# Block 1's modulation vectors: from TensorE matmuls to multiply-and-sum on VectorE, with layer A's first projections advanced tile by tile

## The chip, the core and the metric

The kernel runs on one NeuronCore of a Trainium2 chip. The metric is the device time of one execution in microseconds; three runs of the kernel before gave 2185.78, 2187.06 and 2189.66 us, median 2187.06. Everything else here comes from one profiled execution.

## The reference, cut to what matters

Two transformer blocks on 256 tokens of width 1024, in fp32. Block 1 has a forgetting-attention layer (A), a mixture of experts, a latent-attention layer (B) and a second mixture of experts. Every sublayer's input is an RMS norm that is scaled and shifted, and its output is gated, by vectors computed from one conditioning vector `c`. These vectors are what the change touches:

```python
c_act = jax.nn.silu(c)                                   # [1, 1024]
for layer in range(2):
    sh1, sc1, g1, sh2, sc2, g2 = split(c_act @ w_mod[layer] + b_mod[layer], 6)   # 6 x 1024
    h = rmsnorm(x, norm_g) * (1 + sc1) + sh1
    x = x + g1 * attention(h)
    h = rmsnorm(x, ffn_norm_g[layer]) * (1 + sc2) + sh2
    x = x + g2 * grouped_moe(h)
# between the layers, for the shared keys and values of layer B:
shift, scale = split(c_act @ kv_w_mod + kv_b_mod, 2)     # 2 x 1024
```

Block 2 works the same way with two conditioning vectors (latent and context), which stay as they are.

## The kernel before, in words

Activations are feature-major: `x` is [128 partitions, 8 tiles, 256 tokens]. Weights stream from HBM in units of [128, 1024] fp32 (512 KB) through one ring of eight buffers `raw`; all these loads are issued by SyncE's queue (L335). A linear layer runs in split precision: `wsplit` (L346) makes of each unit a rounded part H on ScalarE (L356) and a remainder L on VectorE (L357), and `lin` (L371) does three matmuls for each of eight tiles of the contraction (L379 to L381).

A modulation is a vector times a matrix. `mods` (L547) does 2048 columns as 16 units: each unit meets `crep`, the activated vector spread over 32 columns, in four matmuls, one to each quarter of the array (L556; each shows as two records in the profile, so 8 records a unit). After 16 units the result is copied (L561), transposed by four matmuls (L564) and added to the bias (L569). One unit is one yield of 1.4.

The order of work is written with generators: `mix` advances several streams in proportion to their yielded amounts against a declared total, and `Chain` strings modulations together so that whoever needs one drives the chain on. In `run` (L1414):

- Layer A: first `drain(mod0([0]))`, the 16 units of shift and scale for layer A's input; then `layer_a` (total 122) mixed with a chain of 80 units (total 115): layer 1's gate and shift group, a group of block 2, the other group of layer 1, another group of block 2, and the group of the shared keys and values.
- Mixture of experts 1: a chain of one group of block 2 and layer 2's first group, then the experts beside the context's work of block 2.
- Layer B: `layer_b` (L1061, total 140) with a chain of layer 2's other 32 units (total 55). Its start is filled with two hidden steps of the context's feed-forward.

`layer_a` (L696) splits `wf` and the first two query tiles ahead, normalises and modulates the whole input (`norm` with `late`, L452, `modulate`, L475), and then runs the three projections one after another, mixed with the chain. The instructions are not issued strictly in the order of the code: the trace has layer A's sums of squares ahead of the first modulation's end, although the code has them after it.

Of the kernel before, what the change touches and what calls it, by code (L numbers as in the profile page):

```python
# [40 lines left out]
# ---------------------------------------------------------------- layout (host)  # L41
# [5 lines left out]
def constants():  # L47
    """Constants that depend on shapes alone: common, of block 1, of block 2, of its even layer."""
# [5 lines left out]
    c1["phalf"] = half  # L54
    c1["ltri"] = (p[:, None] < p[None, :]).astype(np.float32)
    z = np.zeros((P, P))
    c1["causal"] = np.concatenate([z, np.where(p[:, None] >= p[None, :], 0.0, NEG)], 1)
    c1["chunk"] = np.concatenate([z, np.where(p[:, None] // 64 >= p[None, :] // 64, 0.0, NEG)], 1)
    c1["delta"] = (p[:, None] % 32 == np.arange(16)[None, :]).astype(np.float32)
# [31 lines left out]
    return cat(c0), cat(c1), cat(c2), cat(c3)  # L91


(C0_OFF, C0), (C1_OFF, C1), (C2_OFF, C2), (C3_OFF, C3) = constants()
# [15 lines left out]
def kunits(w, kt):  # L110
    """[K, M] -> [K/(128*kt), 128, kt*M]."""
# [5 lines left out]
def modunits(w):  # L117
    """[1024, C] -> [C/2048, 8, 2, 128, 1024]: columns 256*(2j+h).. of four column groups j."""
# [4 lines left out]

def vunits(w):
    """[1024, M] -> [M/256, 2, 128, 4*256]: halves of the contraction."""
# [6 lines left out]
    ("c", 8), ("c2", 8), ("cc2", 8),  # L132
# [13 lines left out]
def layout(i):  # L146
# [6 lines left out]
    for r in range(0, P, 32):  # L153
        bf[r:r + 16, 0] = g["a_b_f"][0]
    vec = {
        "c": cols(g["c"][0]), "c2": cols(g["c_2"][0]), "cc2": cols(g["c_ctx_2"]),
# [18 lines left out]
    # layer A  # L175
# [20 lines left out]
    # layer B  # L196
# [5 lines left out]
    # experts  # L202
# [4 lines left out]
    # block 2, even layer: heads in pairs (i of kv head 0, i of kv head 1)  # L207
# [9 lines left out]
    # block 2, odd layer  # L217
# [12 lines left out]
    o["cst3"] = C3  # L230
    return o
# [32 lines left out]
def upto(n, g):  # L264
    """as much of a generator as amounts to n."""
# [22 lines left out]
class Net:  # L288
# [163 lines left out]
    def norm(self, x, kt, g, sc, sh, dh=None, dl=None, keep=None, save=None, late=False):  # L452
        """rms norm of x [128, kt, 256], times g*(1+sc), plus sh; in parts to dh, dl, or whole to keep; late: sc and sh
        come after x."""
        if late:
            self.modulate(self.normed(x, kt), self.gains(kt, g, sc), sh, dh, dl)
            return
# [1131 lines left out]
```

## Time and profile before

| | us |
|---|---|
| median of three runs | 2187.06 |
| span of the profiled execution | 2181.0 |
| TensorE busy in it | 2045.4 (94%) |
| VectorE busy | 1194.1 (55%) |
| ScalarE busy | 826.0 (38%) |
| GpSimd busy | 138.1 (6%) |
| mean DMA rate | 226 GB/s |

The page gives the span from the first to the last instruction; the execution's own device time is not listed beside it, so the median stands for it, 6.06 us (0.28%) above the span. Busy shares are averages over stages with different limits; the table of stretches says which engine is full where. By the stretches, layer A lies in 0 to about 240 us, the first mixture of experts up to about 700, layer B up to about 915, the second mixture up to about 1290, and block 2 follows.

### The profile page before, as it was taken

The numbers are of one execution on the slowest core, as the hardware profiler recorded it, in microseconds if no ns is written. First come the engines' busy times: TensorE is split into PE (matmuls) and PEld (weight loads), VectorE is DVE, ScalarE is ACT, GpSimd is POOL, SyncE is SP. The second block draws the span as 40 slices with busy tenths as digits, with TensorE's granted clock in tenths as the row PEclk, the third lists the DMA queues.
The fourth block names the chain that finished last, engine by engine and source line by source line (L and its number), as shares of the span: only waits on it lengthen the run. The fifth ranks groups of instructions, "written<-read, shape, count | busy, mean of one in ns | idle before, by whom it ended". The sixth has DMA issues, their size and how long they took to land.

```text
span 2181.0 us, 35834 instructions
## 1 busy us (share of the span) xinstructions
PE 2045.4 (94%) x13942; PEld 1482.8 (68%) x13942; DVE 1194.1 (55%) x3145; ACT 826.0 (38%) x1532; POOL 138.1 (6%) x152
## 2 busy tenths in 40 slices
PE   5999889999998999989999999997999999998999
PEld 3666654444445877783555448766999877768999
DVE  3644643333244676761233247867777555576776
ACT  2443323333123455541121134665444434444443
POOL 1000200000002020100000013102000100001000
PEclk8999889999999999999999999998999999998999
DMA  9788677758787566447877996302655443324552
GB/s 374 267 304 311 248 261 308 267 214 328 293 347 280 203 224 223 144 166 314 360 287 298 409 359 215 134 21 79 211 184 173 158 145 115 113 102 135 185 186 95
DMA packets 135848, 492.87 MB, mean 226 GB/s; under 512 B 15136, under 2 KB 15536, under 8 KB 135408
## 3 DMA queue, kind: packets, MB, share of 16 engines
q1 hardware_dynamic: 134640, 487.63, 61.4%
q8 instruction: 114, 1.87, 0.3%
q10 hardware_dynamic: 864, 2.53, 0.3%
q0 software_dynamic: 160, 0.27, 0.1%
q14 instruction: 70, 0.57, 0.1%
HBM read 489.32 MB, written 1.05 MB: 225 GB/s over the span
## 4 chain that ended last, share of the span: by engine, by line
PE 49%; DVE 3%; ACT 1%; DMA 1%; issue 1%; POOL 0%; SPq 0%; POOLq 0%; ACTq 0%; DVEq 0%
PE psL L379 8%; PE psL L381 8%; PE psL L380 8%; PE psE L931 6%; PE psE L949 2%; PE psM L556 1%; PE psS L1381 1%; PE psT L636 1%; PE psS L1276 1%; PE psD L379 1%; PE psD L381 1%; PE psD L380 1%; PE psV L614 1%; PE psL L393 1%; PE psL L395 1%; PE psL L394 1%
## 5 line engine op out<-in xcount | busy, mean ns | idle before, releaser
L379 PE MATMUL psL<-hh,H 128*128 128x256 f32 (+1 forms) x1800 | 533.8, 298 | 14.4 <-ACT H L356 6.1
L381 PE MATMUL psL<-hh,L 128*128 128x256 f32 (+1 forms) x1800 | 524.2, 293 | 5.3 <-DVE L L357 5.3
L380 PE MATMUL psL<-hl,H 128*128 128x256 f32 (+1 forms) x1800 | 523.2, 292 | 4.1 <-DVE hl L483 3.8
L357 DVE TENSOR_TENSOR L<-raw,H 128x1024 fp32r<-128x1024 f32 (+1 forms) x336 | 410.3, 1225 | 183.0 <-ACT H L356 181.3
L356 ACT CAST H<-raw 128x1024 fp32r<-128x1024 f32 (+1 forms) x336 | 347.1, 1039 | 390.3 <-PE psL L380 123.1
L379 PEld LDWEIGHTS psL<-hh,H 128*128 128x128 f32 x1800 | 350.0, 195 | 58.1 <-issue 25.3
L381 PEld LDWEIGHTS psL<-hh,L 128*128 128x128 f32 x1800 | 348.4, 194 | 32.0 <-issue 16.4
L380 PEld LDWEIGHTS psL<-hl,H 128*128 128x128 f32 x1800 | 349.2, 194 | 15.4 <-issue 4.5
L931 PE MATMUL psE<-eraw,xg 128*64 128x512 f32 x512 | 155.1, 617 | 8.5 <-PEq L997 8.5
L436 POOL TENSOR_TENSOR sa<-sa,sq 128x256 f32<-128x256 f32 x83 | 76.7, 924 | 1215.7 <-ACT sq L434 1210.0
L931 PE MATMUL psE<-raw,xg 128*64 128x512 f32 x512 | 145.3, 603 | 0.0
L556 PE MATMUL psM<-raw,crep 128*32 128x256 f32 x1408 | 126.2, 408 | 15.9 <-DVE crep L606 13.7
L589 ACT ACTIVATE pr<-psS,nm,hr 128x512 f32<-128x512 f32 (+1 forms) x96 | 67.7, 706 | 100.4 <-DVE nm L583 57.8
L949 PE MATMUL psE<-raw,at 128*64 128x512 f32 x384 | 100.0, 599 | 5.4 <-ACT at L943 5.3
L379 PE MATMUL psL<-ah,H 128*128 128x256 f32 x296 | 87.1, 297 | 4.8 <-DVE x L1165 1.3
L380 PE MATMUL psL<-al,H 128*128 128x256 f32 x296 | 84.3, 285 | 0.7 <-DVE al L369 0.7
L381 PE MATMUL psL<-ah,L 128*128 128x256 f32 x296 | 83.8, 284 | 0.3 <-DVE L L357 0.3
L931 PEld LDWEIGHTS psE<-eraw,xg 128*64 128x64 f32 x512 | 38.7, 139 | 64.7 <-issue 54.0
L580 DVE TENSOR_REDUCE mx<-psS 128x1 f32<-128x512 f32 (+1 forms) x80 | 46.1, 580 | 58.6 <-PE psS L1276 44.4
L556 PEld LDWEIGHTS psM<-raw,crep 128*32 128x32 f32 x1408 | 38.9, 113 | 54.9 <-issue 16.5
L931 PEld LDWEIGHTS psE<-raw,xg 128*64 128x64 f32 x512 | 37.0, 136 | 54.2 <-issue 45.2
L955 DVE SCALAR_TENSOR_TENSOR mh<-psE,wsl,mh 128x512 fp32r<-128x512 f32 x32 | 23.3, 747 | 82.5 <-ACT mh L954 82.0
(404 smaller groups left out, 3474.8 us busy)
## 6 DMA issues: line engine op xcount, KB each, us to landing
raw<-in_mod_dram SPq DMA_DIRECT2D x192, 512.0 KB, 4.8
raw<-in_ed_dram SPq DMA_DIRECT2D x96, 512.0 KB, 8.3
raw<-in_fg_dram SPq DMA_DIRECT2D x66, 512.0 KB, 4.4
raw<-in_fu_dram SPq DMA_DIRECT2D x66, 512.0 KB, 4.2
raw<-in_fo_dram SPq DMA_DIRECT2D x66, 512.0 KB, 4.1
eraw<-in_eg_dram SPq DMA_DIRECT2D x64, 512.0 KB, 7.7
raw<-in_eg_dram SPq DMA_DIRECT2D x64, 512.0 KB, 9.2
raw<-in_eu_dram SPq DMA_DIRECT2D x64, 512.0 KB, 7.6
```

The lines of the kernel that those rows point to most:

```text
L356: nc.scalar.copy(h[:, :n], r[:, :n])
L357: nc.vector.tensor_tensor(l[:, :n], r[:, :n], h[:, :n].bitcast(F32), op=ALU.subtract)
L379: mm(ps[:, ns], wh, xh[:, k, ns], start=k == 0, stop=False)
L380: mm(ps[:, ns], wh, xl[:, k, ns], start=False, stop=False)
L381: mm(ps[:, ns], wl, xh[:, k, ns], start=False, stop=k == kt - 1)
L436: (nc.vector if i else nc.gpsimd).tensor_tensor(acc[i], acc[i], sq, op=ALU.add)
L556: nc.tensor.matmul(ps[32 * j:32 * j + 32, 256 * hf:256 * hf + 256], crep[:, k, :], r[:, 256 * j:256 * j + 256], start=k == 0, stop=k == KD ...
L580: V.reduce_max(mx, ps[:, :n], axis=AX.X)
L589: nc.scalar.activation(p, ps[:, :n], AF.Exp, bias=nm, scale=scale, accum_out=sm)
L931: nc.tensor.matmul(ps[64 * j:64 * j + 64, :], xg[:, 2 * q + k, sl[j]], r[j][:, 512 * k:512 * k + 512], start=q + k == 0, stop=q + k == 4)
L949: nc.tensor.matmul(py[hf][64 * j:64 * j + 64, :], at[:, k, 64 * j:64 * j + 64], r[j][:, 512 * hf:512 * hf + 512], start=k == 0, stop=k == 3)
L955: V.scalar_tensor_tensor(yl[:, fs], py[hf], wsl[:, pr:pr + 1], yh[:, fs].bitcast(F32), op0=ALU.mult, op1=ALU.subtract)
```

## The change

All seven groups of block 1 (16 units each, 112 units) leave `mods`. The host stores these weights transposed, so that a unit [128, 1024] holds 128 output features on partitions and the whole contraction along the free dimension; the bytes are the same. A new `rowmods` multiplies each such row unit by the activated vector, which is broadcast to all partitions once, sums it, scales it and adds the bias in one VectorE instruction with an accumulator output, straight into the column of the modulation vector. The norm gains are folded into bias and scale (`gained`), so `norm` gets the finished gain.

```diff
+def rows(w):
+    return np.ascontiguousarray(w.T).reshape(-1, P, D)
...
-    o["mod0"] = modunits(g["w_mod"][0])
-    o["mod1"] = modunits(g["w_mod"][1])
-    o["modkv"] = modunits(g["kv_w_mod"])
+    o["crow"] = np.ascontiguousarray(g["c"].reshape(1, D))
+    o["mod0"] = rows(g["w_mod"][0])
+    o["mod1"] = rows(g["w_mod"][1])
+    o["modkv"] = rows(g["kv_w_mod"])
...
+    def rowmods(self, src, tiles, out, bias, gain=None):
+        V = self.nc.vector
+        for f in tiles:
+            r = self.wload(src[f])
+            one = slice(f, f + 1)
+            sc = 1.0 if gain is None else gain[:, f % KD:f % KD + 1]
+            V.tensor_tensor_reduce(r, r, self.crow, op0=ALU.mult, op1=ALU.add, scale=sc,
+                                   scalar=bias[:, one], accum_out=out[:, one])
+            yield 1.4
+
+    def gained(self, bias, at, g):
+        b = bias[:, at:at + KD]
+        self.nc.vector.scalar_tensor_tensor(b, b, 1.0, g, op0=ALU.add, op1=ALU.mult)
```

Layer A's 16 first row units alternate scale and shift, feature tile by feature tile; then each tile of the input is modulated and all three first projections take one step of the contraction with it (in PSUM banks of kinds V and L):

```diff
-        self.ahead(*((w, KD, P) for w in (a["wf"], a["wqk"][0], a["wqk"][1])))
-        self.norm(self.x, KD, self.v["ang"], m0[:, 8:16], m0[:, 0:8], xh, xl, late=True)
+        self.consts(self.st, "csta", CA, CA_OFF)
+        z = self.normed(self.x, KD)
+        firsts = [(a["wf"], "V"), (a["wqk"][0], "L"), (a["wqk"][1], "L")]
+        ws, pss = [], []
+        for k in range(KD):
+            drain(self.rowmods(a["mod0"], (KD + k,), m0, self.v["bm0"], self.v["ang"]))
+            drain(self.rowmods(a["mod0"], (k,), m0, self.v["bm0"]))
+            if k < len(firsts):
+                ws.append(self.wsplit(firsts[k][0], KD, P))
+                pss.append(self.psum(firsts[k][1]))
+        for k in range(KD):
+            self.modulate(z[k:k + 1], m0[:, KD + k:KD + k + 1], m0[:, k:k + 1], xh[:, k:k + 1], xl[:, k:k + 1])
+            for w, ps in zip(ws, pss):
+                self.lin_k(ps, *(v[:, k] for v in w), xh, xl, k, KD)
         yield 4.0
-        ps = self.lin(self.wsplit(a["wf"], KD, P), KD, xh, xl, S)
+        ps = pss.pop(0)
...
-                ps = self.lin(self.wsplit(a["wqk"][2 * u + m], KD, P), KD, xh, xl, S)
+                ps = pss.pop(0) if pss else self.lin(self.wsplit(a["wqk"][2 * u + m], KD, P), KD, xh, xl, S)
```

`lin_k` is one step of `lin`'s loop. The chains are dealt out anew: block 2's second group (on TensorE) moves from layer A to the first mixture of experts, the keys' and values' vectors move to the experts, and all of layer 2's vectors are made in layer B:

```diff
-            self.crep = self.silu_cols(["c"], self.b1)
+            self.crow = self.b1.tile([P, D], F32, name="crow")
+            nc.sync.dma_start(self.crow, a["crow"].partition_broadcast(P))
+            nc.scalar.activation(self.crow, self.crow, AF.Silu)
...
-                chain = Chain(("gate", mod0([1])), ("c0", mod20([0])), ("m0", mod0([2])), ("c1", mod20([1])),
-                              ("kv", self.mods(a["modkv"], [0], self.crep, self.v["bkv"], mk)))
-                drain(mod0([0]))
+                chain = Chain(("gate", mod0(2)), ("c0", mod20([0])), ("m0", mod0(3)), ("m0", mod0(4, v["ffng0"])),
+                              ("m0", mod0(5)))
...
-                drain(mix((self.layer_a(m0, chain), 122), (chain.run(), 115)))
+                drain(mix((self.layer_a(m0, chain), 122), (chain.run(), 67)))
...
-                chain = Chain(("c2", mod20([2])), ("m1", mod1([0])))
+                chain = Chain(("c1", mod20([1, 2])))
...
-                drain(mix((experts, 196), (then(con, cffn.run(1)), 76)))
+                drain(mix((experts, 196), (then(con, cffn.run(1)), 76), (then(kvmod(0), kvmod(1, v["kvng"])), 23)))
...
-                chain = Chain(("m1", mod1([1, 2])))
-                drain(mix((self.layer_b(mk, m1, chain, cffn.run(3)), 140), (chain.run(), 55)))
+                chain = Chain(("in", mod1(0)), ("in", mod1(1, v["bng"])), ("m1", mod1(2)), ("m1", mod1(3)),
+                              ("m1", mod1(4, v["ffng1"])), ("m1", mod1(5)))
+                drain(mix((self.layer_b(mk, m1, chain, cffn.run(3)), 140), (chain.run(), 67)))
```

In `layer_b`, a `yield from chain.run("in")` stands just before layer B's input is scaled. In the diff `mod0(t)`, `mod1(t)` and `kvmod(t)` are `rowmods` over eight row units, 1024 features. Some constants get tiles of their own in the layer that needs them, and two scratch tiles of block 2 move to another pool.

## Rows read from the trace of the kernel before

**Rows 1.** The page: busy time of each engine, share of the span, instructions.
```profile
PE 2045.4 (94%) x13942; PEld 1482.8 (68%) x13942; DVE 1194.1 (55%) x3145; ACT 826.0 (38%) x1532; POOL 138.1 (6%) x152
```

**Rows 2.** Stretches: length, then busy us of each engine, clock, DMA share, GB/s.
```profile
13.70:32.20 18.50, 13.77 (x140) 6.68 (x140) 2.48 (x13) 2.24 (x6) 5.07 (x7) 0.82 1.03 410
32.20:55.00 22.80, 16.31 (x128) 11.18 (x128) 15.52 (x40) 11.46 (x18) 0.00 (x0) 0.78 1.01 397
60.00:240.00 180.00, 172.45 (x1480) 125.16 (x1484) 94.96 (x270) 71.06 (x152) 5.75 (x6) 0.99 0.80 289
330.00:700.00 370.00, 358.36 (x1726) 173.39 (x1722) 140.42 (x408) 118.97 (x239) 10.22 (x12) 1.00 0.77 296
700.00:750.00 50.00, 46.21 (x371) 41.27 (x371) 28.94 (x53) 14.98 (x21) 7.75 (x9) 0.97 0.56 187
750.00:800.00 50.00, 48.87 (x405) 43.09 (x405) 46.06 (x94) 27.04 (x49) 11.48 (x12) 1.00 0.63 212
800.00:850.00 50.00, 46.51 (x340) 36.16 (x338) 30.79 (x85) 26.77 (x55) 4.69 (x5) 1.00 0.75 243
850.00:915.00 65.00, 63.70 (x457) 49.05 (x456) 48.30 (x187) 34.42 (x97) 2.73 (x2) 1.00 0.44 148
```

**Rows 3.** The same for the modulation matmuls of L556 alone: TensorE, its weight loads.
```profile
60.00:240.00 180.00, 46.67 (x566) 14.60 (x570) 0.99 0.80 289
```

**Rows 4.** TensorE in order of time, layer A: start, us, instruction, count.
```profile
150.52 0.28 PE L395 MATMUL psL<-H,hl 128*128 128x256 f32 x1
150.73 2.37 PE L556 MATMUL psM<-raw,crep 128*32 128x256 f32 x40
153.03 0.33 PE L621 MATMUL psT<-cst,pr 128*128 128x128 f32 x1
...
217.67 0.28 PE L379 MATMUL psL<-oh,H 128*128 128x256 f32 x1
217.78 0.28 PE L380 MATMUL psL<-ol,H 128*128 128x256 f32 x1
217.99 0.64 PE L556 MATMUL psM<-raw,crep 128*32 128x256 f32 x8
218.56 0.39 PE L381 MATMUL psL<-oh,L 128*128 128x256 f32 x1
```

**Rows 5.** VectorE in order of time, layer B.
```profile
755.79 1.22 DVE L357 TENSOR_TENSOR L<-raw,H 128x1024 fp32r<-128x1024 f32 x1
756.93 0.42 DVE L511 TENSOR_TENSOR raw<-raw,psN 128x256 f32<-128x256 f32 x1
...
857.42 0.43 DVE L577 CUSTOM_DVE_ANT_0 psS<-psS,cst 128x256 f32<-128x256 f32 x1
857.76 0.14 DVE L577 DVE_READ_ACCUMULATOR2_ANT mx<- 128x1 f32 x1
857.76 0.95 DVE L357 TENSOR_TENSOR L<-raw,H 128x768 fp32r<-128x768 f32 x1
```

**Rows 6.** Every engine in order of time, the start, to the third projection's read.
```profile
12.84 0.42 ACT L434 ACTIVATE sa<-x 128x256 f32<-128x256 f32 x1 [4.57 <-DMA x<-in_xin_dram]
30.75 0.69 DVE L561 COPY msb<-psM 128x512 f32<-128x512 f32 x1 [8.60 <-PE psM L556]
46.80 0.48 DVE L707 TENSOR_SCALAR fz<-psL,vec 128x256 f32<-128x256 f32 x1 [2.73 <-PE psL L381]
55.13 0.77 ACT L735 ACTIVATE qz<-psL 64x256 f32<-64x256 f32 x2 [3.28 <-PE psL L381]
61.19 0.41 PE L380 MATMUL psL<-hl,H 128*128 128x256 f32 x1
61.40 0.41 PE L381 MATMUL psL<-hh,L 128*128 128x256 f32 x1
```

**Rows 7.** Waits in 60 to 240 us: who waited for whom, us, times, longest.
```profile
ACT pr L589 <- DVE nm L583: 26.5, 14, 5.5
ACT pt L625 <- PE psT L623: 26.1, 15, 3.5
```

More of the change, by code (lines that the diff above doesn't have):

```diff
@@ L89, in cat @@
         return off, np.ascontiguousarray(np.concatenate(cols, 1))
-    return cat(c0), cat(c1), cat(c2), cat(c3)
-(C0_OFF, C0), (C1_OFF, C1), (C2_OFF, C2), (C3_OFF, C3) = constants()
+    return cat(c0), cat(c1), cat(c2), cat(c3), cat(ca), cat(cb)
+(C0_OFF, C0), (C1_OFF, C1), (C2_OFF, C2), (C3_OFF, C3), (CA_OFF, CA), (CB_OFF, CB) = constants()
 def cols(v):
@@ L131 @@
 VEC = [
-    ("c", 8), ("c2", 8), ("cc2", 8),
+    ("c2", 8), ("cc2", 8),
     ("ang", 8), ("kvng", 8), ("bng", 8), ("ffng0", 8), ("ffng1", 8), ("fing", 8),
@@ L230, in layout @@
     o["cst3"] = C3
+    o["csta"] = CA
+    o["cstb"] = CB
     return o
@@ L324, in pools, with consts @@
             setattr(self, n, es.enter_context(self.tc.tile_pool(name=n, bufs=b)))
+    def consts(self, pool, name, v, off):
+        t = pool.tile([P, v.shape[1]], F32, name=self.nm(name))
+        self.nc.scalar.dma_start(t, self.a[name])
+        self.c.update({k: t[:, o:o + w] for k, (o, w) in off.items()})
     def splits(self, es, more, side=None):
@@ L382, in lin, with lin_k @@
         return ps
+    def lin_k(self, ps, wh, wl, xh, xl, k, kt):
+        mm = self.nc.tensor.matmul
+        mm(ps[:, :S], wh, xh[:, k], start=k == 0, stop=False)
+        mm(ps[:, :S], wh, xl[:, k], start=False, stop=False)
+        mm(ps[:, :S], wl, xh[:, k], start=False, stop=k == kt - 1)
     def lin_t(self, ws, kt, n, xh, xl, t0):
@@ L429, in rms @@
         nc = self.nc
-        acc = [self.t(self.sm, [P, S], f"sa{i}", bufs=1) for i in range(len(scales))]
+        acc = [self.t(self.wk if i else self.sm, [P, S], f"sa{i}", bufs=1) for i in range(len(scales))]
         for k in range(kt):
@@ L450, in spread, with norm @@
         return pr[:, :S]
[L452 to L457, printed above, removed]
+    def norm(self, x, kt, g, sc, sh, dh=None, dl=None, keep=None, save=None):
         ga = self.gains(kt, g, sc)
@@ L782, in moe_route @@
         h = self.t(mo, [P, KD, S], "mh")
-        self.norm(x, KD, g, m[:, 32:40], m[:, 24:32], keep=h)
+        self.norm(x, KD, m[:, 32:40], None, m[:, 24:32], keep=h)
         yield 4.0
@@ L1093, in layer_b @@
         self.ahead(*((a["wdq"][m], KD, P) for m in range(2)))
+        yield from chain.run("in")
         z = self.room(KD)
-        self.scale(self.x, KD, self.gains(KD, self.v["bng"], m1[:, 8:16]), z, nc.gpsimd)
+        self.scale(self.x, KD, m1[:, 8:16], z, nc.gpsimd)
         self.affine(z, rs, KD, m1[:, 0:8], xh, xl)
@@ L1460, in run @@
             mk = self.b1.tile([P, 16], F32, name="mk")
-            mod0 = lambda g: self.mods(a["mod0"], g, self.crep, self.v["bm0"], m0)
-            mod1 = lambda g: self.mods(a["mod1"], g, self.crep, self.v["bm1"], m1)
+            v = self.v
+            for b, at, g in (("bm0", 8, "ang"), ("bm0", 32, "ffng0"), ("bkv", 8, "kvng"), ("bm1", 8, "bng"),
+                             ("bm1", 32, "ffng1")):
+                self.gained(v[b], at, v[g])
+            mod0 = lambda t, g=None: self.rowmods(a["mod0"], range(8 * t, 8 * t + 8), m0, v["bm0"], g)
+            mod1 = lambda t, g=None: self.rowmods(a["mod1"], range(8 * t, 8 * t + 8), m1, v["bm1"], g)
+            kvmod = lambda t, g=None: self.rowmods(a["modkv"], range(8 * t, 8 * t + 8), mk, v["bkv"], g)
             with ExitStack() as es:
```

21 lines of the change are left out of this document (11 added, 10 removed).

## The prediction, made before the changed kernel ran

> **What bounds the kernel now.** I read the page first: TensorE is busy 94% of the span, VectorE 55% [rows 1]. An average hides stages, so the table of stretches comes next. In layer A's steady part, 60 to 240 us, TensorE has 172.45 of 180 us and VectorE 94.96; in the experts, 330 to 700, 358.36 of 370 and 140.42; in layer B's four stretches from 700 to 915 together 205.3 of 215 and 154.1 [rows 2]. TensorE is the full engine in all of them. Two places differ. From 13.7 to 55 us the transfers run at 410 and 397 GB/s, a DMA share of about 1, and TensorE is busy about three quarters: the start is bound by loading. And in 750 to 800 us VectorE is busy 46.06 of 50 us: layer B's head is nearly full on both engines. Third, I took the modulation matmuls alone: 46.67 us of TensorE's time in 60 to 240 [rows 3].
>
> **What one unit costs, on either engine.** Removed: a unit of four matmuls. Standing alone between two steps of an accumulation it moves the next matmul from 217.78 to 218.56, 0.78 us where a step is 0.11: 0.67 us. Five in a row take 153.03 - 150.52 - 0.12 = 2.39, or 0.48 each [rows 4]. I take 0.57, between them, since both patterns occur. Added: one VectorE instruction over 1024 elements, in a form that the trace has only narrower. A subtract of 1024 holds the engine 1.14 us, start to start; the multiply-type operation with accumulator, 256 wide, holds it 0.34 and its accumulator read starts together with the next instruction [rows 5]. So 1.14 us a row unit; with the read's 0.14 added to it 1.28 at most. In engine time 1.14 on VectorE replaces 0.57 on TensorE: the exchange pays only where TensorE is the bound and VectorE has room.
>
> **The start: -8 us (-13 to +1).** Before, the sixteen units end at 30.75 us, the forget gates are read at 46.80 and the third projection at 55.13 [rows 6]. After, the bytes ahead of that point are 16 row units (8.39 MB), three weights (1.57), x (1.05), c's broadcast (0.52) and constants (about 0.45): 12.0 MB, 29 us at 410 GB/s, and with the slow first microseconds some 33. VectorE has to do 16 x 1.14 rows, 3 x 1.14 splits, 8 x 0.34 for the norm, 16 x 0.34 for the modulating and about 2 us of small steps: 18.2 + 3.4 + 2.7 + 5.4 + 2 = 32 us. When c's row has landed and passed ScalarE the trace does not show; x, next in line, is first used at 12.84 [rows 6], so VectorE begins between 9 and 13 us and is done at 41 to 45. It, not the loading, is last. Then comes the last tile's nine matmuls. If TensorE keeps up, this is 1 to 2 us (a step is 0.12 us, or 0.21 at the lower clock, as at 61.19 us [rows 6]) and the third projection is ready at 43 to 47. If all 72 matmuls stand behind the row sums, they take 72 x 0.21 = 15 us from about 36, so 51; with 5 us more for a late c row, 56. I take 47: -8. The chain's ten units that ran before 60 us become about six rows, 7 us of VectorE in time that was idle or shorter now.
>
> **Layer A's steady part: -28 us (-38 to 0).** Its window holds 566 records, 71 units; 16 stay on TensorE (block 2's first group), so 36.1 of the 46.67 us go and TensorE keeps 136.4. VectorE gets 32 x 1.14 = 36.5 and has 131.4, with the copies after each group gone (about 3). If TensorE stays as full as it is (172.45 of 180) the window is 142: -38. But VectorE would then be 92% busy, as full as in 750 to 800 us, and its instructions run in order: a row sum stands ahead of splits and of the softmax steps that ScalarE waits for (26.5 us in this window [rows 7]). I take 152 us, TensorE 90% and VectorE 86%. The end at 0 is the case in which the modulations only filled gaps (below). SyncE's queue issues 32 units less here, 16 of them to layer B and 16 to the experts, so loading eases from 289 GB/s.
>
> **First experts: +2 us (0 to +8).** Block 2's group takes the place of layer 2's first group, 16 units for 16. The sixteen key and value rows add 18 us to VectorE's 140.42 of 370, in time that it has idle, and 8.4 MB, which lifts 296 GB/s to 319. They pass through the ring that the experts' weights use, on the same SyncE queue; a row sum whose load is late holds the expert steps behind it on VectorE. 8 us is half a microsecond for each.
>
> **Layer B: +2 us (-18 to +30).** TensorE loses 32 x 0.57 = 18 us, which leaves 187; VectorE gains 48 x 1.14 = 55 and comes to 208.9 of 215. Here VectorE becomes the fuller engine. By stretches, with twelve rows for each 50 us: 42.6 of 50 in 700 to 750 (gain 4, as TensorE allows), 59.8 in 750 to 800 (loss 6 to 10, some rows being done ahead), 44.5 in 800 to 850 (gain 4), about 64 of 65 in the last (0 to +2). The new wait for the input's vectors has little left to do by then: that point is reached after about 39 of 140 declared units, where the chain has made 13 of its 16 rows; the three others cost VectorE 3.4 us in its fullest place, with the scaling on GpSimd and the query-side projections behind them. Worst, a row stands in front of what TensorE needs next all the time: 55 less part of the 18.
>
> **The sum.** -8 - 28 + 2 + 2 = -32 us. The profiled execution's span is 2181.0 us and the median of the runs 2187.06, 0.28% more; I keep those 6.06 us as they are: 2149 for the span, 2155 for the time.
>
> **The rivals.** *All of it comes back* (2118): TensorE bounds every stage and VectorE's rows find idle time; -13 - 38 + 0 - 18 = -69. For it: 94% and 55%. Against: the sum for layer B, 97% of VectorE.
>
> *The modulations were filler* (2183): TensorE without them waits for the softmax chain instead. For it: the five units at 150.73 run just after the values' projection ended and right before the transposes of finished weights [rows 4], and ScalarE waits 26.1 us for transposes, 26.5 us for VectorE [rows 7]. Against: elsewhere units sit between steps at the full pace of 0.12 us, where each one delays the rest. Layer A then gives nothing and the sum is -8 + 0 + 2 + 2 = -4. The Trainium skill speaks for this rival in "Perfetto Trace Analysis", section "Identifying the Most-Contended Engine": matmul busy time does not tell how close TensorE is to its limit, and the weight loads' busy share is the better measure. By that page, the 125.16 us of weight loads in 180 (70%) [rows 2] would leave TensorE headroom in layer A, and the 32 us would shrink to 4.
>
> *VectorE takes over* (2218, the slower side): in layers A and B each of the 80 row sums sits ahead of a split or softmax step that TensorE waits for. Price 80 x 1.14 = 91, less TensorE's relief of 36 + 18, -8 and +2: +31. It decides from the point where VectorE's share goes beyond the 92% of 750 to 800 us, in which TensorE was still busy 48.87 of 50 us. For it: 208.9 of 215 in layer B. Against: that same stretch, and the 131 of 152 in layer A.
>
> *The tiles don't advance together* (2164): the modulating stays behind all sixteen row sums and the projections start as late as now; the start gives +1 and the rest stands.
>
> **How the numbers follow.** Forecast 0.52, all back 0.14, filler 0.17, VectorE 0.12, no advance 0.05. A measurement of this kernel tells about 0.2% (4.4 us) from no change. Filler, at 4 us, is split 0.07 faster, 0.09 same, 0.01 slower; the other cases fall on one side each: faster 0.52 + 0.14 + 0.05 + 0.07 = 0.78, same 0.09, slower 0.13. The time is the forecast's, 2155. The forecast alone spans about 2135 to 2175; for 8 in 10 the range reaches up past the filler to 2190 and down to 2118, which leaves out VectorE's case and half of the first.
>
> **What would show it.** In the profile after: row sums of about 1.14 us from one to the next; 16 of them before about 35 us, and the third projection's read near 47; layer A's output projection over near 205 instead of 240, with VectorE at 85 to 90% and TensorE near 90%; waits of TensorE for the remainder of a split (L357) or for softmax steps grown in layer B, and VectorE above 92% there. The forecast is wrong if TensorE in layer A falls below 85% busy while VectorE stays below it too (filler), if a row sum costs well over 1.3 us, or if TensorE's waits for VectorE add more than 20 us from 700 to 915.

## The result, and the profile after

The changed kernel takes 2219.03 us (median of 2216.17 to 2220.61) against 2187.64 of the kernel before on the same chip: 1.0141 times, 95% interval 1.0127 to 1.0156. The prediction was 2155. The busy line of its page:

```profile
PE 2003.7 (90%) x13018; PEld 1485.1 (67%) x13018; DVE 1312.8 (59%) x3354; ACT 828.9 (37%) x1532; POOL 141.9 (6%) x152
```

Against [rows 1] TensorE has 41.7 us less to do and VectorE 118.7 more, as meant, and the span is 37.8 us longer. The same stretches as in [rows 2] (length; busy us of PE, PEld, DVE, ACT, POOL; granted clock, DMA share, GB/s):

```profile
13.70:32.20 18.50, 3.95 (x13) 3.07 (x13) 10.04 (x27) 4.15 (x7) 4.39 (x7) 1.00 0.50 189
32.20:55.00 22.80, 11.53 (x53) 10.07 (x52) 22.18 (x40) 4.54 (x7) 0.00 (x0) 0.85 0.96 344
60.00:240.00 180.00, 151.01 (x1110) 125.19 (x1110) 141.78 (x393) 87.12 (x183) 12.83 (x14) 0.91 0.70 238
330.00:700.00 370.00, 350.59 (x1693) 172.83 (x1690) 157.45 (x422) 111.93 (x221) 12.23 (x13) 0.99 0.82 313
700.00:750.00 50.00, 40.98 (x300) 38.98 (x298) 38.77 (x71) 14.98 (x20) 5.61 (x8) 0.93 0.71 241
750.00:800.00 50.00, 39.43 (x282) 36.95 (x282) 44.88 (x89) 21.87 (x40) 13.66 (x10) 0.90 0.53 169
800.00:850.00 50.00, 36.54 (x208) 33.05 (x209) 40.06 (x88) 21.99 (x40) 3.98 (x5) 0.80 0.66 219
850.00:915.00 65.00, 54.11 (x330) 41.73 (x328) 57.80 (x197) 33.15 (x88) 4.85 (x4) 0.92 0.61 205
```

At the start loading falls from 410 to 189 GB/s and VectorE is full from 32 us on. In layer B neither TensorE (40.98, 39.43, 36.54 of 50) nor VectorE is full. The row sums, grouped (busy us, mean ns, idle before):

```profile
L595 DVE CUSTOM_DVE_ANT_0 raw<-raw,crow,vec 128x1024 f32<-128x1024 f32 x112 | 144.9, 1302 | 15.4 <-DMA raw<-in_modkv_dram 11.5
```

Where the time goes is read best from landmarks that both kernels have: the first start of the forget gates' step on ScalarE (before: 47.3 us), of the routed tokens' first transpose (249.6), of the zeroing of layer B's keys (699.7), the last addition of layer B's output projection (923.2), and the span's end. How much later or earlier each comes than before, and the difference from one to the next, gives each stage's loss (+) or gain in us. So the column "first experts" also holds the routing and the other work ahead of the first expert's matmul. The runs of the next section stand in the same table; the ratio is that of the times to before.

| kernel | start | layer A | first experts | layer B | the rest | ratio |
|---|---|---|---|---|---|---|
| changed | +13.1 | -36.2 | +20.9 | +30.6 | +9.4 | 1.0141 |
| narrow_rows | +3.8 | -43.8 | +16.2 | -1.8 | +8.9 | 0.9882 |
| rows_no_load | +7.0 | -36.5 | +2.0 | -9.2 | +6.2 | 0.9827 |
| tiny_loads | +13.8 | -48.5 | +6.6 | +25.2 | +11.2 | 0.9994 |
| rows_and_units | +15.0 | -24.8 | +17.9 | +39.4 | +6.9 | 1.0235 |
| rows_first | +10.0 | -38.8 | +22.0 | +30.1 | +9.8 | 1.0127 |
| start_rows | +10.2 | +1.7 | +5.6 | -1.2 | +7.2 | 1.0046 |
| advance_only | +0.4 | +1.8 | +6.0 | -0.2 | -2.9 | 1.0010 |
| a_chain_rows | +2.9 | -8.6 | +2.9 | -1.0 | +8.6 | 1.0001 |
| a_chain_kv_rows | +2.3 | -7.0 | +5.9 | -0.9 | +4.5 | 1.0022 |
| kv_rows_ahead | +3.1 | -14.4 | +15.9 | -1.1 | +1.4 | 1.0000 |
| second_rows_ahead | +3.3 | -0.2 | -1.8 | -1.1 | +4.6 | 0.9981 |
| b_32_rows | +2.5 | -0.9 | -1.6 | +4.0 | +3.4 | 1.0000 |
| rows_in_quarters | +13.3 | -35.8 | +17.9 | +47.5 | +9.6 | 1.0174 |
| scratch_back | +12.1 | -34.1 | +17.0 | +34.3 | +6.3 | 1.0108 |
| eighty_rows | +2.3 | -8.1 | +0.5 | +6.3 | +3.2 | 1.0009 |

Each line is one profiled execution, and executions of one kernel differ by some 4 us either way (second_rows_ahead: 2182.02 to 2190.53), so cells below 4 us are no evidence. In every run that lists it, the profiled execution's time lies 1.74 to 1.84 us above its span. By that, the profiled execution of before took about 2182.8 us, 4 to 5 less than its median, and the lines' sums are that much too high: six runs with ratios near 1 (a_chain_rows to b_32_rows, and eighty_rows) show +2 to +3 us at the start and +1 to +9 in "the rest".

### The profile page after: what moved, and what is told of

It reads as the page before. It is cut to its first block, busy times and chain, and to the rows that moved or that the text cites. A ratio compares the mean times of both kernels' runs of the same rounds, so it can differ in the third digit from the quotient of the medians.

```text
span 2218.8 us, 34196 instructions
## 1 busy us (share of the span) xinstructions
PE 2003.7 (90%) x13018; PEld 1485.1 (67%) x13018; DVE 1312.8 (59%) x3354; ACT 828.9 (37%) x1532; POOL 141.9 (6%) x152
## 3 DMA queue, kind: packets, MB, share of 16 engines
q8 instruction: 106, 1.74, 0.3%
## 5 line engine op out<-in xcount | busy, mean ns | idle before, releaser
L595 DVE CUSTOM_DVE_ANT_0 raw<-raw,crow,vec 128x1024 f32<-128x1024 f32 x112 | 144.9, 1302 | 15.4 <-DMA raw<-in_modkv_dram 11.5
L976 PEld LDWEIGHTS psE<-eraw,xg 128*64 128x64 f32 x512 | 39.4, 139 | 62.9 <-issue 53.2
L393 PEld LDWEIGHTS psL<-ah,H 128*128 128x128 f32 x296 | 58.2, 198 | 24.7 <-DVE sil L1226 8.4
L1000 DVE SCALAR_TENSOR_TENSOR mh<-psE,wsl,mh 128x512 fp32r<-128x512 f32 x32 | 23.3, 748 | 81.2 <-ACT mh L999 80.7
L1226 DVE TENSOR_TENSOR sil<-psL,sil 128x256 f32<-128x256 f32 x66 | 27.9, 423 | 68.2 <-PE psL L395 67.1
```

The lines of the kernel that those rows point to most:

```text
L393: mm(ps[:, ns], wh, xh[:, k, ns], start=k == 0, stop=False)
L595: V.tensor_tensor_reduce(r, r, self.crow, op0=ALU.mult, op1=ALU.add, scale=sc, scalar=bias[:, one], accum_out=out[:, one])
L976: nc.tensor.matmul(ps[64 * j:64 * j + 64, :], xg[:, 2 * q + k, sl[j]], r[j][:, 512 * k:512 * k + 512], start=q + k == 0, stop=q + k == 4)
L1000: V.scalar_tensor_tensor(yl[:, fs], py[hf], wsl[:, pr:pr + 1], yh[:, fs].bitcast(F32), op0=ALU.mult, op1=ALU.subtract)
L1226: nc.vector.tensor_tensor(s, pu[:, :S], s, op=ALU.mult)
```

## The experiments

The theories were these. *VectorE*: the row sums stand ahead of, or crowd out, what TensorE waits for. *Loads*: what hurts is the 8.4 MB of each sixteen row tiles, moved to other stages. *Filler*: TensorE's units were never on the path, so taking them away gives nothing. *Clock*: TensorE has more gaps in layer B and is granted less there (0.80 to 0.93 in the four stretches, 0.97 to 1.00 before), and the lower clock costs the time.

**The sums' time or the loads' bytes.** Sums over an eighth, with all loads:

```diff
-            V.tensor_tensor_reduce(r, r, self.crow, op0=ALU.mult, ...
+            V.tensor_tensor_reduce(r[:, :P], r[:, :P], self.crow[:, :P], op0=ALU.mult, ...
...
```

> The changed kernel with every row sum taken over 128 of its 1024 elements: all 112 row tiles are still loaded whole, in their places, but VectorE has about 112 x 1.05 = 118 us less to do (seven eighths of each sum are left out, so the modulations are other numbers; the branch for full experts is kept from being taken). If VectorE's time is the cause, the start gets back its 13 us, the first experts their 21 and layer B its 31, and TensorE's relief in layer B (18) shows too: about 2140 us. If the cause is the loads (16 row tiles moved from layer A into the experts, 16 more into layer B, and their places in the ring), the lags of the experts and of layer B stay at 15 us or more each and the time is 2200 or more.

2164.87 us, ratio 0.9865 to 0.9899, between the two times expected. The start gets back 9 of its 13 us, layer B all of its 31; the first experts keep 16 of 21. Full sums without loads:

```diff
-            r = self.wload(src[f])
-            V.tensor_tensor_reduce(r, r, self.crow, ..., scale=sc,
+            V.tensor_tensor_reduce(self.crow, self.crow, self.crow, ..., scale=0.0,
...
```

> The changed kernel with all 112 row sums at their full 1024 elements, but over a tile that stays in the chip: no row tile is loaded (58.7 MB less), the ring and SyncE's queue are free of them, VectorE's time is as in the changed kernel (the vectors are the biases alone; the branch for full experts is kept from being taken). If VectorE's time is the cause, the first experts still lose 15 us or more and layer B 25 or more against the kernel before, and only the start gains a few: 2205 or more. If the loads are the cause, the start gives back about 13, the experts 20 and layer B 20 or more: about 2165.

2152.39 us (0.9811 to 0.9844), but it answers another question: without loads nothing held the sums back, and in VectorE's order all of them stand early. The sums' busy time by stretch (length, DVE, clock, DMA share, GB/s):

```profile
70.00:260.00 190.00, 69.35 (x109) 0.90 0.57 189
260.00:330.00 70.00, 45.09 (x70) 0.85 0.60 218
330.00:500.00 170.00, 0.01 (x1) 0.99 0.74 268
```

None is left in the experts or layer B. So it shows what these stages cost without any row sum and any row tile: +2.0 and -9.2. To hold the sums in place, each keeps its ring tile, loaded with 16 of 1024 columns:

```diff
-            r = self.wload(src[f])
+            r = self.wload(src[f][:, :16], 16)
-            V.tensor_tensor_reduce(r, r, self.crow, ..., scale=sc,
+            V.tensor_tensor_reduce(r, self.crow, self.crow, ..., scale=0.0,
...
```

> The changed kernel with 16 of each row tile's 1024 columns loaded (0.9 MB in place of 58.7), the sums still over 1024 elements (of c's row, which stays in the chip) and written into the loaded tile, so that each keeps its place in the ring, in SyncE's queue and on VectorE behind its own load; the vectors are the biases alone, and the branch for full experts is kept from being taken. If the experts' 21 us are the 8.4 MB of rows in that stage, they fall to 5 or less. In layer B, if VectorE's time is the cause, 20 us or more of the 31 stay; if it is the loaded bytes, under 8 stay; the row sums without loads (all of them ran before 330 us there) left this open. In all: 2185 to 2205 by VectorE, about 2160 by the bytes.

2187.42 us (0.9985 to 1.0004). Layer B keeps 25 of 31 us, and the start all of its 13: there it is VectorE. The experts keep 7 of 21: here the loads matter (the account below says where). Layer B in narrow_rows and then in tiny_loads, whole:

```profile
676.00:897.00 221.00, 196.16 (x1365) 176.77 (x1366) 169.66 (x514) 106.60 (x226) 33.13 (x33) 0.94 0.68 232
```
```profile
672.00:920.00 248.00, 209.39 (x1367) 186.90 (x1368) 209.16 (x514) 107.32 (x226) 44.75 (x33) 0.88 0.37 109
```

The second moves about half as much, and is 27 us longer with 39.5 us more of VectorE's work.

**What TensorE's units are worth.** The removed matmuls put back beside 80 row sums, on resident data:

```diff
+            if fill:
+                ps = self.psum("M")
+                for j in range(4):
+                    self.nc.tensor.matmul(ps[32 * j:32 * j + 32, 0:256], self.crep2[:, 0, :],
+                                          self.crow[:, 256 * j:256 * j + 256], ...)
...
```

> The changed kernel with, beside each of the 80 row sums of layer 1's and layer 2's vectors that go on beside layers A and B, four matmuls of 32x256 on resident data whose results are dropped: what the removed units did on TensorE (80 x 0.57 = 46 us) with no load of its own. If TensorE is what these stages wait for, 46 us more: 2265. If they wait for VectorE, the matmuls fall into gaps: 2219 to 2229. If part of the loss is TensorE's clock, which goes down to 0.80 to 0.93 in layer B when it has gaps, the added work keeps the clock up and the time falls, by 8 us or more: 2211 or less.

2240.66 us (1.0218 to 1.0252): 21.6 us for 58.6 us more of TensorE's busy time (2062.3 on its page, 2003.7 above). Against the changed kernel layer A loses 11.4 (0.36 us a unit), layer B 8.8 (0.18); with some 4 us of scatter in each profile these are rough, and they are prices in a TensorE that is busy 84% and 82% of these stages (151.01 of 180 us, 205.25 of 251). A lower clock doesn't explain layer B: from 708 to 970 us it is now 0.95 (0.89 in the changed kernel from 700 to 960), and the stage is longer. Then the exchange itself, layer A's 32 units alone as row sums, everything else as before:

```diff
-                chain = Chain(("gate", mod0([1])), ("c0", mod20([0])), ("m0", mod0([2])), ("c1", mod20([1])), ...
+                chain = Chain(("gate", mod0(2)), ("c0", mod20([0])), ("m0", mod0(3)), ("m0", mod0(4)),
+                              ("m0", mod0(5)), ("c1", mod20([1])), ("kv", kvmod()))
```

> One part of the change alone: the 32 units of layer A's gate and second half as row sums beside layer A; the start's 16 units, the key and value units, and layer 2's 48 units are matmuls on TensorE as before, where they were before. If TensorE is what layer A waits for, 32 x 0.57 = 18 us go: 2169. Putting such matmuls back beside both layers' rows cost 11 us in layer A, so by that run 2176. If the matmuls only filled gaps, or a row sum delays what TensorE needs next, 2185 or more.

2189.63 us, 0.9991 to 1.0010: nothing, though its layer A is 8.6 us shorter in the profiled execution. With the sixteen key and value units as rows too:

```diff
-            kvmod = lambda: self.mods(a["modkv"], [0], self.crep, v["bkv"], mk)
+            kvmod = lambda: self.rowmods(a["modkv"], range(16), mk, v["bkv"])
```

> As the kernel with layer A's 32 units as row sums, and the sixteen key and value units too, beside layer A, where their matmuls were. TensorE loses 16 x 0.57 = 9 us more in layer A; VectorE gets 16 x 1.27 = 20 and comes to about 95 + 61 = 156 of some 160 us there. If VectorE has room, 5 to 9 us less than with 32 rows; if 97% is too full for it, as layer B's head suggests, 5 us more or worse.

2193.46 us (1.0012 to 1.0032): nine more us off TensorE gain nothing, the kernel is 4 us slower.

**The start.** The loop over the sums moved ahead of the norm of x:

```diff
-        z = self.normed(self.x, KD)
         firsts = [(a["wf"], "V"), (a["wqk"][0], "L"), (a["wqk"][1], "L")]
         ws, pss = [], []
         for k in range(KD):
             ...
+        z = self.normed(self.x, KD)
```

> The changed kernel with one move at the start: the loop over the first sixteen row sums and the three first weights is written ahead of the norm of x, so the rows take the ring's places and VectorE's queue before the norm's steps. If the start's 13 us come from the norm standing ahead of the rows (first row sum at 25.83 us, loading held up from 13 to 27), the forget gates' reads come 8 to 13 us earlier than in the changed kernel and the time is 2206 to 2211. If VectorE's sum of work there is the bound in any order, it stays within 3 us of 2219.

2218.26 us (1.0100 to 1.0154), the start 3 us better and the time as in the changed kernel. VectorE in order of time, first in the changed kernel, then here (start, us, instruction):

```profile
24.83 1.07 DVE L489 TENSOR_TENSOR raw<-x,psN 128x256 f32<-128x256 f32 x3
25.83 1.33 DVE L595 CUSTOM_DVE_ANT_0 raw<-raw,crow,vec 128x1024 f32<-128x1024 f32 x1
27.09 0.08 DVE L595 DVE_READ_ACCUMULATOR2_ANT m<- 128x1 f32 x1
27.09 1.28 DVE L595 CUSTOM_DVE_ANT_0 raw<-raw,crow,vec 128x1024 f32<-128x1024 f32 x1
...
57.42 1.27 DVE L595 CUSTOM_DVE_ANT_0 raw<-raw,crow,vec 128x1024 f32<-128x1024 f32 x1
58.62 0.08 DVE L595 DVE_READ_ACCUMULATOR2_ANT m<- 128x1 f32 x1
58.62 0.47 DVE L752 TENSOR_SCALAR fz<-psV,vec 128x256 f32<-128x256 f32 x1
```
```profile
11.78 1.35 DVE L595 CUSTOM_DVE_ANT_0 raw<-raw,crow,vec 128x1024 f32<-128x1024 f32 x1 [4.03 <-DMA raw<-in_mod_dram]
...
49.37 0.75 DVE L500 TENSOR_TENSOR hl<-sq,hh 128x256 fp32r<-128x256 f32 x2
50.04 1.27 DVE L595 CUSTOM_DVE_ANT_0 raw<-raw,crow,vec 128x1024 f32<-128x1024 f32 x1
...
54.87 1.28 DVE L595 CUSTOM_DVE_ANT_0 raw<-raw,crow,vec 128x1024 f32<-128x1024 f32 x1
56.07 0.08 DVE L595 DVE_READ_ACCUMULATOR2_ANT m<- 128x1 f32 x1
56.07 0.47 DVE L752 TENSOR_SCALAR fz<-psV,vec 128x256 f32<-128x256 f32 x1
```

The first sum comes 14 us earlier and the last modulated tile 7 us earlier (49.37 for 57.08), but then five sums for the gate stand ahead of the forget gates' short step on VectorE, from 50.04 to 56.07. The start alone as changed, in the kernel before (its layer_a with the row sums and the advance, its other vectors on TensorE):

```diff
-                drain(mod0([0]))
+            drain(self.rowmods(a["mod0r"], (KD + k,), m0, self.v["bm0"], self.v["ang"]))
+            drain(self.rowmods(a["mod0r"], (k,), m0, self.v["bm0"]))
...
```

> The kernel before with the start alone as changed: the first sixteen units as row sums on VectorE, and the tiles advancing; everything behind is on TensorE as before, where it was. If VectorE's sum of work in the start is what made it late, the forget gates' reads come 10 to 14 us later than before and that lag stays through layer A, where nothing was taken from TensorE: 2197 to 2201. If layer A makes it up, 2190 or less.

2200.91 us, 1.0031 to 1.0060: 11 us lost and not made up later. The other half of that edit, the tiles advancing with three projections while the vectors stay on TensorE:

```diff
+        for k in range(KD):
+            self.modulate(z[k:k + 1], ga[:, k:k + 1], m0[:, k:k + 1], xh[:, k:k + 1], xl[:, k:k + 1])
+            for w, ps in zip(ws, pss):
+                self.lin_k(ps, *(v[:, k] for v in w), xh, xl, k, KD)
```

> The other part of the change alone, on the kernel before: all vectors stay on TensorE, but layer A's input is modulated tile by tile while the forget gates and the first two query projections advance with each tile. If it does what it says, the third projection's read (55.13 us before) comes near 47 to 50, since only one tile's matmuls are left after the last modulated tile, and the whole is 5 to 8 us faster: about 2181. If the tail of matmuls is hidden or the lead is lost again in layer A, within 3 us of before: 2187.

2192.35 us (1.0002 to 1.0019). The first query projection is read at 47.45 us (51.10 before) and the second, the third projection of the prediction, at 50.28 (55.13 before), the forget gates' no earlier than before, and nothing is left of it by the end of layer A.

**Layer A and the first experts.** The key and value units as rows, moved from layer A to the stretch ahead of the first experts:

```diff
-                chain = Chain(("c2", mod20([2])), ("m1", mod1([0])))
+                chain = Chain(("kv", kvmod()), ("c2", mod20([2])), ("m1", mod1([0])))
```

> The kernel before with only the sixteen key and value units as row sums, and moved: out of layer A, where TensorE is full, to the stretch ahead of the first experts, where VectorE is busy 41.8 of 90 us and the loads run at 257 GB/s. By the price of a unit in layer A (11/32 = 0.36 us) 6 us go there, 8.4 MB of loads leave it too, and if the stretch ahead of the experts takes both in, 2178 to 2184. If that stretch grows by as much (its loads and row sums stand ahead of the first experts' weights), 2188 to 2195.

2188.61 us, 0.9991 to 1.0010: layer A is 14.4 us shorter, the experts 15.9 longer. Layer 2's first sixteen as rows in the place that they had:

```diff
-                chain = Chain(("c2", mod20([2])), ("m1", mod1([0])))
+                chain = Chain(("c2", mod20([2])), ("m1", self.rowmods(a["mod1r"], range(16), m1, v["bm1"])))
```

> The kernel before with only layer 2's first sixteen units as row sums, in the place they had (ahead of the first experts, from about 296 to 327 us): the same bytes in the same stage, VectorE about half idle there (41.8 of 90 us from 240 to 330). If the exchange pays where VectorE has room and the loads stay put, up to 16 x 0.57 = 9 us: 2178 to 2184. If TensorE has slack there too (72.3 of 90 us), 2185 to 2190.

2185.84 us, 0.9971 to 0.9990: 4 us faster than before, and the fastest of the runs that leave nothing out.

**Layer B.** The 48 sums there cut into quarters, each handing its partial sum on:

```diff
+            n = 4 if src is self.a["mod1"] else 1
+            for i in range(n):
+                d = out[:, one] if i == n - 1 else self.t(self.sm, [P, 1], "rq", bufs=4)
+                V.tensor_tensor_reduce(r[:, c], r[:, c], self.crow[:, c], ..., scalar=acc, accum_out=d)
```

> The changed kernel with each of layer 2's 48 row sums cut into four sums over 256 elements that hand the partial sum on; loads, places and everything else as in the changed kernel. A quarter holds VectorE about 0.34 us, so a row takes 1.36 or somewhat more in place of 1.27, and the order of VectorE's queue may put short steps (the steps of a reciprocal root, a softmax's maximum) between quarters. If a row sum hurts by standing in front of such steps, layer B's loss of 31 us falls to 18 or less: 2206 or less. If it is VectorE's total, the loss stays or grows with the 5 us and more of added time: 2219 to 2230.

2229.29 us (1.0158 to 1.0189): layer B loses 47.5 instead of 30.6. A quarter's mean is 500 to 514 ns, not the 340 expected, so the 48 rows take 96.8 us of VectorE instead of 62.4. The stage gets 17 us longer for these 34, so the run can't tell whether the finer interleaving alone gives something back. Fewer sums in the stage, the first sixteen ahead of the experts and 32 beside layer B:

```diff
-                chain = Chain(("m1", mod1([1, 2])))
+                chain = Chain(("m1", self.rowmods(a["mod1r"], range(16, 48), m1, v["bm1"])))
```

> The kernel before with layer 2's 48 units as row sums, 16 of them ahead of the first experts (where their matmuls were) and 32 beside layer B; start, layer A and the key and value vectors on TensorE as before. By the prices from the runs in layer B (a row sum 32/48 = 0.68 us, a unit of TensorE 9/48 = 0.18) layer B loses 32 x 0.5 = 16, and the sixteen ahead of the experts give 4: about 2201. If VectorE costs only from some share on (97% was foreseen with 48, about 88% with 32), layer B loses 5 or less: 2185 to 2191.

2190.81 us, 0.9991 to 1.0009: layer B loses 4.0. So 32 sums cost almost nothing, and the sixteen more of the changed kernel, which its layer B needs for its own input, 27. What these sixteen do is seen in the changed kernel, every engine in order of time (the bracket: idle before it, and who ended that):

```profile
776.14 10.48 POOL L521 TENSOR_SCALAR raw<-x,m 128x256 f32<-128x256 f32 x6 [70.19 <-DMA raw<-in_mod_dram]
...
783.66 1.27 DVE L595 CUSTOM_DVE_ANT_0 raw<-raw,crow,vec 128x1024 f32<-128x1024 f32 x1
783.80 0.70 PE L680 MATMUL psN<-ro,cstb 128*128 128x256 f32 x2 [1.99 <-DVE ro L1133]
784.86 0.08 DVE L595 DVE_READ_ACCUMULATOR2_ANT m<- 128x1 f32 x1
784.86 0.41 DVE L684 TENSOR_TENSOR ro<-psN,sin 128x256 f32<-128x256 f32 x1
...
787.29 1.82 POOL L521 TENSOR_SCALAR raw<-x,m 128x256 f32<-128x256 f32 x2
...
789.08 0.72 POOL L682 TENSOR_TENSOR ro<-ro,cos 128x256 f32<-128x256 f32 x1
789.83 0.42 DVE L686 TENSOR_TENSOR ro<-ro,ro 128x256 f32<-128x256 f32 x1 [4.23 <-POOL ro L682]
790.18 0.42 DVE L528 TENSOR_TENSOR raw<-raw,rs 128x256 f32<-128x256 f32 x1
790.51 0.48 DVE L539 SCALAR_TENSOR_TENSOR hl<-raw,m,hh 128x256 fp32r<-128x256 f32 x1
...
791.05 0.58 PE L394 MATMUL psL<-hl,H 128*128 128x256 f32 x1 [2.03 <-DVE hl L539]
```

GpSimd's scaling of x by these vectors starts only at 776.14, just behind a row sum (its accumulator is read at 775.79) and 10.4 us later than before:

```profile
765.73 7.63 POOL L504 TENSOR_SCALAR raw<-x,ga 128x256 f32<-128x256 f32 x8 [57.56 <-DVE L L357]
```

The rotary product for the keys (L682) is queued on GpSimd behind it until 789.08; VectorE waits 4.23 us for that with the tiles of the query side queued behind on its own queue, and TensorE is busy 2.35 of the 9 us from 782 to 791. That is the new wait. From the latent's copy (777.1 in both kernels) to the last copy of the query's down projection (819.9, before 806.0) the stage loses 13.9 us. From 777.1 to 806 TensorE has four long waits (us, times, longest); before it has none over 0.5 us there:

```profile
PE psN L469 <- DVE nr L435: 5.6, 1, 5.6
PE psN L461 <- POOL sa L457: 2.9, 1, 2.9
PE psL L394 <- DVE hl L539: 2.0, 1, 2.0
PE psN L680 <- DVE ro L1133: 2.0, 1, 2.0
```

The second and third, 4.9 us, come through GpSimd's queue: a sum of squares and the rotary product stand there behind the scalings. In the first and the last, 7.6 us, row sums stand in VectorE's queue among the short steps that TensorE waits for: one (781.98) ahead of the copy of the keys' part, and three (798.93, 800.95, 802.61) among the steps of the latent's reciprocal root:

```profile
796.22 0.15 DVE L442 TENSOR_SCALAR nv<-psN 128x2 f32<-128x2 f32 x1
...
798.93 1.27 DVE L595 CUSTOM_DVE_ANT_0 raw<-raw,crow,vec 128x1024 f32<-128x1024 f32 x1
...
802.61 1.28 DVE L595 CUSTOM_DVE_ANT_0 raw<-raw,crow,vec 128x1024 f32<-128x1024 f32 x1
...
804.20 0.16 DVE L435 SCALAR_TENSOR_TENSOR nr<-nu,nr 128x2 f32<-128x2 f32 x1
```

Of the rest of the 31 us, 2 come before 777.1 and 14 to 15 after 819.9, where the changed kernel has 25 sums still to do; b_32_rows, which began with its 32 at 713, has 16 left at the same copy (809.0).

**Two that close the account.** The double norm's scratch tiles back in their old pool:

```diff
-        acc = [self.t(self.wk if i else self.sm, [P, S], f"sa{i}", bufs=1) for i in range(len(scales))]
+        acc = [self.t(self.sm, [P, S], f"sa{i}", bufs=1) for i in range(len(scales))]
...
-        r = self.t(self.wk, [P, S], "r1")
+        r = self.t(self.sm, [P, S], "r1", bufs=1)
```

> The changed kernel with the two scratch tiles of the double norm at block 2's start back in the pool where they were before. If their move is what costs 6 us there (lag +28.0 to +34.0 us from the last expert to the first normed tile), 2213; if the lag there comes from the state of the ring and the queues, 2219 as it is.

2215.47 us (1.0086 to 1.0130), against the changed kernel's 1.0127 to 1.0156: 3.6 us by the medians and 7 by the ratios, at the edge of what the runs can tell. From the last expert to block 2's first use of x on GpSimd the loss is 2.0 us, where the changed kernel has 6.0. And all pieces that cost little, together: layer A's 32 (as in a_chain_rows), layer 2's first sixteen ahead of the experts, 32 beside layer B:

```diff
-                chain = Chain(("c2", mod20([2])), ("m1", mod1([0])))
+                chain = Chain(("c2", mod20([2])), ("m1", mod1(0, 16)))
...
-                chain = Chain(("m1", mod1([1, 2])))
+                chain = Chain(("m1", mod1(16, 48)))
```

> The kernel before with 80 of the 112 units as row sums, each in the place of its matmuls: layer A's 32 beside layer A, layer 2's first sixteen ahead of the first experts, its other 32 beside layer B; the start's sixteen and the key and value units stay on TensorE. If each stage takes row sums at no cost up to its VectorE's limit, it is what the parts gave: 0 for layer A's, -4 for the sixteen, +4 for layer B's, so 2186 to 2192. If VectorE's work in one stage holds up the next, 2200 or more. If TensorE's 80 x 0.57 = 46 us were on the path, they show now: 2160 or less.

2191.20 us, 1.0000 to 1.0018. Its busy line:

```profile
PE 2008.1 (92%) x13282; PEld 1478.6 (68%) x13282; DVE 1275.3 (58%) x3295; ACT 828.8 (38%) x1534; POOL 142.5 (7%) x152
```

TensorE does 37.3 us less than in [rows 1] and VectorE 81.2 more, and the time is the same. So the exchange as such gives nothing. Two reasons would look alike here: the units only filled gaps, or the sums cost what the units gave. rows_and_units speaks for a mixture (a unit was worth 0.36 and 0.18 of its 0.57 us); no run takes units away from the kernel before without putting sums in their place.

## Why the prediction was wrong, step by step

**What bounds the kernel.** This is the step that failed first. TensorE's 94%, and 172.45 of 180 in layer A [rows 1, 2], were taken to mean that each microsecond off TensorE is a microsecond off the end. rows_and_units prices a unit at 0.36 us in layer A and 0.18 in layer B, where the sum had 0.57, and eighty_rows took 37.3 us off TensorE for nothing. The prediction's own sign for filler is there too: from 60 to 240 us TensorE is 84% busy and VectorE 79%. The five units that ran while the array had just finished one product and was about to transpose [rows 4] pointed that way; the rival that said so was given 0.17. The Trainium skill says in "Perfetto Trace Analysis", section "Identifying the Most-Contended Engine", that matmul busy time doesn't tell the headroom, and that the weight loads' share does better, beside the share of peak arithmetic. The first half agrees with eighty_rows; the second isn't tested here, since the weight loads' share is 68% before and in eighty_rows and 67% in the changed kernel, which took 31 us longer.

This step alone would have left the time near 2183. By size the miss lies in three other terms of the sum, the start, the first experts and layer B, put at -8, +2 and +2 and measured at +13, +21 and +31.

**The price of a row: 1.14 us.** From a sum's start to the next instruction it is 1.19 to 1.43 us, 1.23 in the mean (busy 1302 ns; the accumulator's read, 80 ns, starts with the next instruction): between the 1.14 and the 1.28 kept as the most it could be. A small miss, 10 us of VectorE over 112 rows.

**The start: -8, measured +13.** VectorE's sum of 32 us was about right: from 25.83 to 58.62 it is busy 31.40 us, with two of the gate's sums in it and the norm's scalings ahead of it. What was wrong is where it begins. "Between 9 and 13 us" took it that the rows go first; they stood behind the norm's scalings, whose reciprocal root waits for TensorE's sums, and the loading stopped for them. Even with the rows first, VectorE needed 38 us to the last tile and then had five more sums ahead of the forget gates. narrow_rows gives 9 of the 13 back. That the tiles advance together came true, and gives nothing that lasts (advance_only). The chain's rows, counted as lying in idle time, are among those that stand in the way: two in the changed kernel, five in rows_first.

**Layer A: -28, measured -36.** The right sign for the wrong reason. The exchange in it, alone, is -8.6 in the profile and nothing in the time. The rest is work sent elsewhere: sixteen units leaving layer A with their loads shorten it by 14 (kv_rows_ahead), and two such groups left. If the second, which no run moves alone, counts like the first, 8.6 + 2 x 14 = 37. The step counted all 55 units as saved, 28 us of their 36.1.

**First experts: +2, measured +21.** The step priced the sixteen rows by VectorE and took the 8.4 MB as free, since 296 GB/s would become 319. It did come to 313, and the stage lost 21 us; with sums an eighth as long 16 remain, with a sixty-fourth of the bytes 7. In kv_rows_ahead the same bytes, with whole sums, cost 15.9 there. But 14 of the 21 lie where none of these rows run: from the routed tokens' first transpose to the first expert's matmul the changed kernel takes 91.2 us (77.5 before), layer A's last sum starts at 207.8, and the first load of a key and value tile is issued at 327.2, ten us after that matmul. tiny_loads has the same 91.2 and then 365.5 us for the experts, where the changed kernel takes 379.8 and before 372.6. So the bytes cost some 14 us among the experts; why the stretch ahead grew was not taken apart (part of the context's work stands there now, 560 matmul records instead of 522). Nor was it taken apart why TensorE's supply suffers so at 82% DMA share: the ring, the queue and the transfer rate all stand between.

**Layer B: +2, measured +31.** The work was counted right: 208.9 us of VectorE foreseen, 209.16 in tiny_loads' layer B. The step that failed is that VectorE could do it in 215 us, at 97%. It was made from one row, 46.06 of 50 us in the stage's busiest stretch; over the whole of layer B it gets to 83 to 87% in every version with this much to do (207.28 of 251 in the changed kernel, 209.16 of 248 in tiny_loads, 190.36 of 223 in b_32_rows, 237.75 of 272 in rows_in_quarters). 208.9 at 0.84, a share known only afterwards, would have been 249, where the stretch took 251 from 700. And the wait for the input's vectors, "little left to do", put at 3.4 us with GpSimd's scaling named behind it, stands in a stretch that loses 14: TensorE's four long waits there are 4.9 us through GpSimd's queue and 7.6 through row sums in VectorE's. That the sums' time on VectorE is the cause of layer B's loss is shown (narrow_rows, tiny_loads); how it divides between this wait and the share is read from the trace, since no run keeps 48 sums in layer B and makes its input's vectors earlier.

**Unforeseen.** The moved scratch cost 3.6 to 7 us, at the edge of the noise. The 6.06 us around the span weren't real (1.8 in all runs): the span read as the base was some 4 us too short for a usual execution.

**The rivals.** *VectorE takes over*, at 0.12, gave 2218, 1 us from the result, but by luck, from a sum that doesn't hold: it had every sum of layers A and B cost 1.14 us. In layer A a sum costs 0.24 (changed against narrow_rows, 7.6 over 32, little more than the scatter), in layer B 0.68 (32.4 over 48), and even that is no price for each, since the 32 of b_32_rows cost 4.0 in all. Its point of decision, VectorE beyond 92%, was too high as well. The forecast's 0.52 should have been lower for one reason that stood in the text: the sum needed VectorE fuller for 200 us than it had been for 50.

## What to carry to other kernels

Before work moves from a busy engine to an idle one, price the busy engine's unit by its effect on the end, for instance by adding such work where its result is dropped: here 0.57 us of TensorE's work, added to the changed kernel, was worth 0.36 us in one stage and 0.18 in another, and taking 37.3 us away for row sums was worth nothing in a kernel whose TensorE was 94% busy. Don't count on the share that the receiving engine reaches in its best stretch for a whole stage, and follow each new result into the queues of the engines that use it. A stage that gets shorter because work left it is no gain until the stage that took the work in, with its bytes, has been counted.

## What the runs showed of the hardware

Cutting a sum of 1024 elements (1302 ns in the mean) into four made 500 to 514 ns each, not a quarter, and 128 elements took 367 (narrow_rows). By the step from 128 to 256, about 140 ns, an estimate from these means is that some 230 ns of each instruction don't depend on its length. In rows_first, while GpSimd was busy 5.91 of the 6.30 us from 13.7 to 20, row sums on VectorE took 1.53 to 1.74 us and the split 1.63, against 1.28 and 1.23 once GpSimd was idle:

```profile
13.26 1.53 DVE L595 CUSTOM_DVE_ANT_0 raw<-raw,crow,vec 128x1024 f32<-128x1024 f32 x1
...
15.63 1.63 DVE L371 TENSOR_TENSOR L<-raw,H 128x1024 fp32r<-128x1024 f32 x1 [0.83 <-ACT H L370]
17.18 1.74 DVE L595 CUSTOM_DVE_ANT_0 raw<-raw,crow,vec 128x1024 f32<-128x1024 f32 x1
...
26.74 1.28 DVE L595 CUSTOM_DVE_ANT_0 raw<-raw,crow,vec 128x1024 f32<-128x1024 f32 x1
```

The transfers ran near their most there too (410 GB/s), but they aren't enough: in the changed kernel a sum takes 1.27 us at 57.42 with 403 GB/s from 57 to 59 and GpSimd idle. GpSimd is slower as well: in the changed kernel its first five scalings from 776.14 on took 1.43 to 2.50 us beside row sums and splits, and the other three 0.92 us each, from 785.70 on, while VectorE waited. The two engines together are slower than each alone here; no run was made to take that apart.
